# A hybrid decoder layer on one Trainium2 core: tiles of the phases, the input's squares, the sums of the left factors and the transposes of the merged rows moved

## The chip, the core and the metric

The kernel runs on one NeuronCore of a Trainium2 chip, in one launch. Five engines work beside each other, each in the order of its own instruction list: PE (TensorE) multiplies and transposes into PSUM, PEld loads its weights, DVE (VectorE) and ACT (ScalarE) do elementwise work, POOL (GpSimd) a little of it, and SP (SyncE) issues most DMAs; ACT's list holds DMA issues too. They wait for each other by semaphores. The metric is the device time of one execution in microseconds (us); here it is the median of three runs.

## The reference

One layer with SEQ = 256 tokens and D_MODEL = 4096, in float32:

```python
h = rms_norm(x, norm_gains)
z = h @ w_in            # GLA q,k,v,gate,decay | SWA q,k,v,gate | merge gates ga, gb
o_a = rms_norm(gla_mix(q, k, v, log_a), gla_norm_gains)    # 8 heads, chunks of 64, o_t = q_t S_t
y_a = (o_a * silu(gg)) @ w_gla_out                         # 2048 x 4096
o_b = swa_sink_mix(sq, sk, sv, sinks)                      # window 128, 32 query and 8 key heads
y_b = (o_b * silu(sg)) @ w_swa_out                         # 2048 x 4096
merged = sigmoid(ga + b0) * y_a + sigmoid(gb + b1) * y_b
x = x + merged @ w_out                                     # 4096 x 4096
return rms_norm(x, final_norm_gain)
```

## The kernel before, in words

**Products.** Every factor is split into a rounded part (hi) and a remainder (lo), and a product is three PE passes: hi·hi, hi·lo, lo·hi. For the weights ACT writes hi (`halves`, a CAST) and DVE writes lo (a TENSOR_TENSOR) for every raw tile of 512 KB that SP has fetched; `STG` (3) or `STM` (5) such hi and lo tiles exist, so a cast of a later tile waits until PE is done with an earlier one. One pass is a matmul of 128 x 128 by 128 x 512.

**Blocks (`gemm`).** The columns of `w_in` but the merge gates come in blocks of 512 (gq, gk, gv, gg for GLA; sk, sv, sq, sg for SWA); a block has 32 k-tiles, two token halves and so 192 matmuls. In the first block, gq, the input is fetched in pieces and `first_inputs` makes from each piece hT (ACT hi, DVE lo, 128 x 256 each, left factor of all blocks) and its squares: ACT squares 128 x 512, POOL adds them into `ssq` (L130).

**Pairs (`pair`).** The five large products (ya and yb out of the branches, ga and gb the merge gates, o the last one) go in pairs of 1024 columns, n = 0 to 3, with steps j of 256 rows of the weight (8 steps for ya and yb, 16 for the others). A step fetches two raw tiles r and s. In eight-form it takes 8 products (24 matmuls) into four accumulators q2, q3, q4, q8. In the steps of `SEVEN` it takes 7 products (21 matmuls): DVE forms sums t, u and s of the weight (L214 to L216), the left factor's sums lie ready in `xc`, and four more accumulators, q1, q5, q6, q7, take part. `combine` makes `xc` with six DVE operations and one ACT cast a step (L172 to L182). Pair 0 of each kind (ya0, yb0, ga0, o0) has eight-form alone, and `combine` stands behind it in the program.

**Ends of a pair (`outputs`).** In eight-form ACT copies the four accumulators (L262). In seven-form ACT copies q1, DVE forms v from q6 and two sums from q5 and q7, a third from q5, and adds q2, q3, q4, q8 (L247). PSUM has eight banks, so the next pair's first matmul into a bank waits until DVE or ACT has read it.

**Stages.** GLA (gq to gg), ya (spilled to DRAM), SWA (sk to sg), yb (spilled), then ga and gb alternately, whose sigmoids gate ya and yb into `m`; then the m stage: 16 groups of four PE transposes of m (m_t, L288), each split into `mT` by an ACT cast (L278) and a DVE subtraction (L279); then o0 to o3 with the residual x (`xt`) and, at the end, the root mean square over a row, the scaling and the writes. Staging tiles and work tiles of a stage lie in pools (`phase`) that are freed for the next; a new tile on the same memory waits for the old one's readers.

**Order.** A list scheduler places the instructions of each engine with its own estimates and the priorities `PRIO` (raw tiles and splits of blocks) and `PRM` (those of pairs); what stands where in a list is therefore not what the source reads like, and is shown below where it matters.

Of the kernel before, what the change touches and what calls it, by code (L numbers as in the profile page):

```python
# [49 lines left out]
def trunk_kernel(  # L50
# [59 lines left out]
    def first_inputs(gp, ssq):  # L110


        def before(k0, n):
# [74 lines left out]
    def pair(name, lhs, w, npr, xc=None, before=None, last=False):  # L188

        sev = SEVEN[npr] if xc is not None else ()  # L190
# [58 lines left out]
    def outputs(q, d, name, pool):  # L249

        if 1 in q:
# [5 lines left out]
            add(d[1][1], q[5], d[1][0], ALU.subtract)  # L257
        for t, i, b in ((0, 0, 2), (0, 1, 3), (1, 0, 4), (1, 1, 8)):
            if 1 in q:
                add(d[t][i], q[b], d[t][i])  # L260
            else:
                nc.scalar.copy(d[t][i], q[b])  # L262

    def spilled(name, lhs, w, dst, xc, pool):
# [237 lines left out]
    with phase("hl2") as cur["hl"], phase("swa") as sp:  # L502
# [35 lines left out]
        for i in range(4):  # L538
            qT = pairsT(f"sq{i}", zblock("sq", i), "qT")
            on = sp.tile([P, NT, NB], F32, tag="on", name=f"on{i}")  # L540
# [95 lines left out]
    mT = big.tile([P, KT, 2, S], F32R, tag="hT", name="mT")  # L636
    xcm = xp.tile([P, len(SEVEN[KT // 2]), 4, 2, P], F32R, tag="xc", name="xcm")
    st = ep.tile([P, NT, NBLK + 1], F32, tag="ev", name="st")
    for j in range(KT // 2):
        transpose_split(mT, 2 * j, m[:, :, 2 * j * P : 2 * (j + 1) * P], 2, f"m{j}")  # L640
    x2 = big.tile([P, NT, DM], F32, tag="oT", name="x2")
    for n in range(NP2):
        last = n == NP2 - 1
# [4 lines left out]
        outputs(q, [[x2[:, t, cs[i]] for i in range(2)] for t in range(NT)], f"o{n}", ep)
        gf = ep.tile([P, 2, NB], F32, tag="bt", name=f"gf{n}")
        nc.scalar.dma_start(gf, gfin[2 * n * NB : 2 * (n + 1) * NB].partition_broadcast(P).rearrange("p (i c) -> p i c", i=2))  # L650
        for t in range(NT):
            for i in range(2):
                xq = x2[:, t, cs[i]]
                xt = ep.tile([P, NB], F32, tag="yr", name=f"xt{n}{t}{i}", bufs=2)
                nc.scalar.dma_start(xt, x[t * P : (t + 1) * P, cs[i]])
                add(xq, xq, xt)
                nc.scalar.activation(xt, xq, AF.Square, accum_out=st[:, t, 2 * n + i : 2 * n + i + 1])  # L657
                add(xq, xq, gf[:, i, :], ALU.mult)
    for t in range(NT):
        sf = st[:, t, NBLK:]  # L660
        nc.vector.tensor_reduce(sf, st[:, t, :NBLK], AX.X, ALU.add)
        rms_scale(sf, sf, DM)
        for c in range(4):
            os = slice(c * 1024, (c + 1) * 1024)
            if c % 2 == 0:
                nc.vector.tensor_scalar(x2[:, t, os], x2[:, t, os], sf, None, ALU.mult)
# [77 lines left out]
```

## Time and profile before

| | us |
|---|---|
| median of 3 runs (2490.53 to 2492.29) | 2490.99 |
| profiled execution, its span | 2495.09, 2493.4 |
| PE busy | 2437.6 (98%), 10986 matmuls |
| DVE, ACT, POOL busy | 1724.6 (69%), 1225.4 (49%), 42.5 (2%) |
| mean DMA rate | 197 GB/s |

The profiled execution took 4.1 us more than the median of the runs, and 1.69 us of it lie around its span. PE is busy nearly all the time, so what can be won lies in matmuls left out, in the stops of PE and in stretches in which its clock is at the lower level.

### The profile page before, as it was taken

What the parts mean: (1) busy time and instruction counts of PE and PEld (TensorE: products, weight loads), DVE (VectorE), ACT (ScalarE), POOL (GpSimd) and SP (SyncE); (2) the same over time, 40 slices, a digit from 0 to 9 for tenths busy, and PEclk for the clock granted to TensorE, in tenths of its full rate; (3) what the DMA queues carried; (4) which work ended last, traced back from release to release, by engine and by line L of the source; (5) the groups of instructions that cost most, each with busy time, mean ns of one, the idle gap of its engine ahead of it and who ended that gap; (6) DMA issues with size and microseconds to landing.
All of it is one profiled execution on the core that took longest, in us unless ns stands there. A gap on an engine that the chain in (4) does not pass through costs nothing.

```text
span 2493.4 us, 29365 instructions
## 1 busy us (share of the span) xinstructions
PE 2437.6 (98%) x10986; PEld 1999.0 (80%) x10986; DVE 1724.6 (69%) x1929; ACT 1225.4 (49%) x1479; POOL 42.5 (2%) x52
## 2 busy tenths in 40 slices
PE   8999999999999999999989999999999999999997
PEld 6788888887877888888878788888888888788886
DVE  7465555445785455555557885799889988968886
ACT  6444444444543444445444444555555555545554
POOL 4000000000000000000000000000000000000000
PEclk9999999999999999999999999999999999999999
DMA  7556556556565655554556675677667676656665
GB/s 250 157 169 192 170 176 194 170 170 204 191 223 183 192 179 160 152 186 152 161 178 193 218 245 185 213 227 228 216 216 227 216 227 216 202 186 216 225 221 191
DMA packets 139024, 491.14 MB, mean 197 GB/s; under 512 B 15840, under 2 KB 16224, under 8 KB 138880
## 3 DMA queue, kind: packets, MB, share of 16 engines
q1 hardware_dynamic: 127296, 461.69, 58.4%
q10 hardware_dynamic: 11584, 27.57, 3.2%
q8 instruction: 86, 1.41, 0.2%
q14 instruction: 58, 0.48, 0.1%
HBM read 476.61 MB, written 12.58 MB: 196 GB/s over the span
## 4 chain that ended last, share of the span: by engine, by line
PE 89%; DVE 5%; issue 2%; DMA 2%; ACT 1%; POOL 0%; SPq 0%; ACTq 0%; POOLq 0%; DVEq 0%
PE ga_q L234 5%; PE ga_q L236 4%; PE ga_q L235 4%; PE gb_q L236 4%; PE gb_q L234 4%; PE gb_q L235 4%; PE o_q L236 4%; PE o_q L235 4%; PE o_q L234 4%; PE sg_a L163 2%; PE sg_a L162 2%; PE sq_a L164 2%; PE sq_a L163 2%; PE sq_a L162 2%; PE sg_a L164 2%; PE gg_a L164 2%
## 5 line engine op out<-in xcount | busy, mean ns | idle before, releaser
L214 DVE TENSOR_TENSOR gb_t<-gb_r,gb_s 128x1024 f32<-128x1024 f32 x24 | 29.3, 1221 | 11.0 <-DMA gb_s<-in_wgate_dram 11.0
L103 POOL TENSOR_TENSOR st<-st,mhalf 128x1 f32<-128x1 f32 x2 | 1.1, 553 | 1700.4 <-DVE st L102 1700.4
L565 ACT ACTIVATE s<-s,mx 128x128 f32<-128x128 f32 x64 | 28.4, 445 | 0.0
L214 DVE TENSOR_TENSOR o_t<-o_r,o_s 128x1024 f32<-128x1024 f32 x18 | 22.0, 1221 | 9.1 <-DMA o_s<-in_wout_dram 9.1
L130 POOL TENSOR_TENSOR ssq<-ssq,sq 128x512 f32<-128x512 f32 x15 | 26.4, 1757 | 25.3 <-ACT sq L129 24.7
L214 DVE TENSOR_TENSOR ga_t<-ga_r,ga_s 128x1024 f32<-128x1024 f32 x18 | 22.0, 1221 | 4.9 <-DMA ga_s<-in_wgate_dram 4.7
L121 DVE SCALAR_TENSOR_TENSOR hT<-xsb,gin_sb,hT 128x256 fp32r<-128x256 f32 x32 | 21.9, 733 | 4.9 <-ACT hT L120 4.9
L550 DVE SCALAR_TENSOR_TENSOR s<-s,mask 128x384 f32<-128x384 f32 x32 | 16.0, 552 | 6.0 <-PE s L549 6.0
L143 ACT CAST sg_16h<-sg_r 128x1024 fp32r<-128x1024 f32 x4 | 4.2, 1056 | 28.0 <-PE sg_a L164 28.0
L214 DVE TENSOR_TENSOR ya_t<-ya_r,ya_s 128x1024 f32<-128x1024 f32 x9 | 11.0, 1222 | 8.6 <-DMA ya_s<-in_wgla_dram 8.6
L214 DVE TENSOR_TENSOR yb_t<-yb_r,yb_s 128x1024 f32<-128x1024 f32 x9 | 11.0, 1222 | 8.4 <-DMA yb_s<-in_wswa_dram 8.4
L657 ACT ACTIVATE xt<-x 128x512 f32<-128x512 f32 x16 | 10.1, 630 | 13.7 <-DVE x L247 13.7
L216 DVE TENSOR_TENSOR gb_s<-gb_u,gb_s 128x512 f32<-128x512 f32 x24 | 16.5, 688 | 0.3
L215 DVE TENSOR_TENSOR gb_u<-gb_t,gb_r 128x512 f32<-128x512 f32 x24 | 16.5, 688 | 0.3
L473 DVE COPY oraw<-op 128x512 f32<-128x512 f32 x8 | 5.5, 692 | 15.6 <-PE op L472 15.6
L582 DVE COPY pT<-pt 128x384 f32<-128x384 f32 x16 | 8.9, 554 | 9.3 <-PE pt L579 9.3
L464 POOL TENSOR_SCALAR_AFFINE_SELECT ats<-ats 128x128 f32<-128x128 f32 x16 | 8.0, 523 | 415.4 <-DVE ats L462 415.4
L476 ACT ACTIVATE jk<-oraw 128x256 f32<-128x256 f32 x16 | 6.7, 418 | 16.9 <-DVE oraw L473 16.6
L579 PEld LDWEIGHTS pt<-ident,s 128*128 128x128 f32 x96 | 11.4, 145 | 4.4 <-ACT s L565 3.9
L120 ACT ACTIVATE hT<-xsb,gin_sb 128x256 fp32r<-128x256 f32 x32 | 14.1, 499 | 1.8 <-DMA xsb<-in_xT_dram 1.2
L579 PE MATMUL pt<-ident,s 128*128 128x128 f32 x96 | 14.9, 278 | 0.0
L288 PE MATMUL m_t<-ident,m 128*128 128x128 f32 x64 | 10.2, 302 | 3.7 <-DVE mT L279 3.7
(2816 smaller groups left out, 8954.8 us busy)
## 6 DMA issues: line engine op xcount, KB each, us to landing
gv_r<-in_win_dram SPq DMA_DIRECT2D x64, 512.0 KB, 3.8
gg_r<-in_win_dram SPq DMA_DIRECT2D x64, 512.0 KB, 4.0
sq_r<-in_win_dram SPq DMA_DIRECT2D x64, 512.0 KB, 3.6
sg_r<-in_win_dram SPq DMA_DIRECT2D x64, 512.0 KB, 3.7
ga_r<-in_wgate_dram SPq DMA_DIRECT2D x64, 512.0 KB, 4.7
ga_s<-in_wgate_dram SPq DMA_DIRECT2D x64, 512.0 KB, 5.1
gb_r<-in_wgate_dram SPq DMA_DIRECT2D x64, 512.0 KB, 4.6
gb_s<-in_wgate_dram SPq DMA_DIRECT2D x64, 512.0 KB, 5.4
```

Source lines behind the costliest of these rows:

```text
L121: nc.vector.scalar_tensor_tensor(hT[:, kt, 1, :], xsb[:, kt, :], g, hT[:, kt, 0, :].bitcast(F32), ALU.mult, ALU.subtract)
L130: nc.gpsimd.tensor_tensor(ssq, ssq, sq, ALU.add)
L162: nc.tensor.matmul(acc[t], lh, hi[:, i, :], start=kt == 0, stop=False)
L163: nc.tensor.matmul(acc[t], lh, lo[:, i, :], start=False, stop=False)
L164: nc.tensor.matmul(acc[t], ll, hi[:, i, :], start=False, stop=kt == nkt - 1)
L214: nc.vector.tensor_tensor(ts, r1, r2[:, 0:1, :].broadcast_to([P, 2, NB]), ALU.add)
L215: nc.vector.tensor_tensor(t2[:, 0, :], ts[:, 1, :], r1[:, 0, :], ALU.add)
L234: nc.tensor.matmul(q[i], lh, hi[:, c, :], start=done[i] == 1, stop=False)
L235: nc.tensor.matmul(q[i], lh, lo[:, c, :], start=False, stop=False)
L236: nc.tensor.matmul(q[i], ll, hi[:, c, :], start=False, stop=done[i] == total[i])
L565: nc.scalar.activation(s4[:, k, cs], s4[:, k, cs], AF.Exp, bias=mx[:, k, t : t + 1], accum_out=sm[:, k, t : t + 1],)
L579: nc.tensor.transpose(tp[:, m * P : (m + 1) * P], s4[:, k, m * P : (m + 1) * P], ident)
```

## The change

The tiles that a stage still needs in its last instructions move to pools of their own: `glo` takes gng_sb, oraw, ss, gt from GLA's pool, `slo` takes on, sg from SWA's. `mixed_staging` claims the staging tiles of ya and yb in a fixed order at the stage's start. The input's squares are emitted inside the second block (gk) instead of the first. Pair 0 of ya, yb and ga takes seven-form from step 5 (ya, yb) or 8 (ga) on, and `combine` is spread over its steps 1 to 3 or 1 to 6. Of the 16 groups of transposes of m, 12 are emitted inside `outputs` of gb3, before its last four sums; the other four come in steps 2 to 5 of o0, and o's `combine` in its steps 9 to 14. In o's pairs x comes in one DMA a pair and is added before the accumulator of the last sum instead of after it. In o3 the products of q8 come last; the scaling of the last 512 columns takes the final gain with it; a row's output goes in six pieces instead of four.

```diff
+        def squares(k0, n):
             xr = xsb[:, k0 : k0 + n, :]
-            if k0 < KW:
-                nc.scalar.activation(ssq[:, k0 : k0 + n, :], xr, AF.Square)
+            if k0 == 0:
+                nc.scalar.activation(ssq, xr, AF.Square)
                 return
...
+    def mixed_staging():
+
+        cur["n"], cur["r"] = STM, 6
+        for tag, n, dt, bufs in (("hi", 2, F32R, STM), ("raw", 2, F32, 6), ("t2", 1, F32, 1), ("t13", 2, F32, 1), ("lo", 2, F32R, STM)):
+            cur["hl"].tile([P, n, NB], dt, tag=tag, name=f"first_{tag}", bufs=bufs)
...
-    def pair(name, lhs, w, npr, xc=None, before=None, last=False):
+    def pair(name, lhs, w, npr, xc=None, before=None, last=False, since=0):
 
-        sev = SEVEN[npr] if xc is not None else ()
+        sev = [j for j in SEVEN[npr] if j >= since] if xc is not None else ()
...
-                work.sort(key=lambda x: x[0] in (4, 8))
+                work.sort(key=lambda x: {4: 1, 8: 2}.get(x[0], 0))
...
+        if between is not None:
+            between()
         for t, i, b in ((0, 0, 2), (0, 1, 3), (1, 0, 4), (1, 1, 8)):
             if 1 in q:
+                if extra is not None:
+                    add(d[t][i], d[t][i], extra[t][i])
                 add(d[t][i], q[b], d[t][i])
+            elif extra is not None:
+                add(d[t][i], q[b], extra[t][i])
             else:
                 nc.scalar.copy(d[t][i], q[b])
 
+    def first_pair(lhs, xc, npr, name, order, since, n):
+
+        if n > 0:
+            return {}
+
+        def before(j):
+            if 1 <= j <= len(order):
+                combine(lhs, xc, SEVEN[npr], name, at=order[j - 1])
+
+        return {"before": before, "since": since}
...
-        q0 = zblock("gq", 0, before=first_inputs(gp, ssq), chunks=RAMP)
-        k0 = zblock("gk", 0)
+        load, squares = first_inputs(gp, ssq)
+        q0 = zblock("gq", 0, before=load, chunks=RAMP)
+        k0 = zblock("gk", 0, before=squares)
...
+    def merged():
+
+        mTs.append(big.tile([P, KT, 2, S], F32R, tag="hT", name="mT"))
+        for j in range(3 * KT // 8):
+            transpose_split(mTs[0], 2 * j, m[:, :, 2 * j * P : 2 * (j + 1) * P], 2, f"m{j}")
...
+    sums = lambda j: (
+        combine(mT, xcm, SEVEN[KT // 2], "m", at=j - 9) if j >= 9
+        else transpose_split(mT, 2 * (j + 10), m[:, :, 2 * (j + 10) * P : 2 * (j + 11) * P], 2, f"m{j + 10}") if 2 <= j < 6
+        else None
+    )
...
+    for t in range(NT):
+        nc.vector.tensor_scalar(sf[t], st[:, t, NBLK - 1 : NBLK], 1.0 / DM, sf[t], ALU.mult, ALU.add)
+        nc.gpsimd.tensor_tensor(sf[t], sf[t], mhalf[:, 0:1], ALU.pow)
+        at = 0
+        for c, w in enumerate((512, 512, 1024, 1024, 512, 512)):
```

**Place one: ACT near the end of the first block.** gq_24h to gq_28h are casts of the first block's weights, hT makes the left factor of the input's pieces, sq are the squares. Before:

```order
L143 CAST gq_24h<-gq_r_420 128x1024
L129 ACTIVATE sq_391<-xsb 128x512
L129 ACTIVATE sq_417<-xsb 128x512
L337 DMA bdec_sb<-in_bdec_dram 128x8
L129 ACTIVATE sq_442<-xsb 128x512
L143 CAST gq_26h<-gq_r_445 128x1024
L120 ACTIVATE hT<-xsb,gin_sb 128x256 x4
L143 CAST gq_28h<-gq_r_471 128x1024
L129 ACTIVATE sq_468<-xsb 128x512
```

With the change:

```order
L145 CAST gq_24h<-gq_r_385 128x1024
L131 ACTIVATE sq_701<-xsb 128x512
L131 ACTIVATE sq_722<-xsb 128x512
L365 DMA gng_sb<-in_gng_dram 128x256
L145 CAST gq_26h<-gq_r_407 128x1024
L120 ACTIVATE hT<-xsb,gin_sb 128x256 x4
L131 ACTIVATE sq_743<-xsb 128x512
L145 CAST gq_28h<-gq_r_430 128x1024
L131 ACTIVATE sq_764<-xsb 128x512
```

The square sq_442, which stood ahead of the cast gq_26h, stands behind that cast and behind the four hT operations (as sq_743); the other squares shown keep theirs, although the source has them in the next block.

**Place two: PE at the passage from SWA to yb.** ob_t are the eight transposes of the last SWA rows, yb_q the accumulators of yb0, yb_r0h and yb_r0l the two parts of its first weights, obT the left factor. Before:

```order
L288 MATMUL ob_t_9266<-ident,on_8819 128x128
L288 MATMUL ob_t_9273<-ident,on_8819 128x128
L288 MATMUL ob_t_9266<-ident,on_8819 128x128 x3
L288 MATMUL ob_t_9273<-ident,on_8819 128x128 x3
L234 MATMUL yb_q_9292<-yb_r0h,obT 128x512
L234 MATMUL yb_q_9294<-yb_r0h,obT 128x512
L234 MATMUL yb_q_9293<-yb_r0h,obT 128x512
L235 MATMUL yb_q_9292<-yb_r0l,obT 128x512
```

With the change (the first row is the first transpose):

```order
L313 MATMUL ob_t_9297<-ident,on_8850 128x128
L313 MATMUL ob_t_9304<-ident,on_8850 128x128
L244 MATMUL yb_q_9333<-yb_r0h,obT 128x512
L244 MATMUL yb_q_9335<-yb_r0h,obT 128x512
L244 MATMUL yb_q_9334<-yb_r0h,obT 128x512
L244 MATMUL yb_q_9336<-yb_r0h,obT 128x512
L245 MATMUL yb_q_9333<-yb_r0l,obT 128x512
L246 MATMUL yb_q_9333<-yb_r0h,obT 128x512
L245 MATMUL yb_q_9335<-yb_r0l,obT 128x512
L313 MATMUL ob_t_9297<-ident,on_8850 128x128 x3
L313 MATMUL ob_t_9304<-ident,on_8850 128x128 x3
L246 MATMUL yb_q_9335<-yb_r0h,obT 128x512
```

Seven matmuls of yb now stand between the second transpose and the other six. On ACT the casts of yb_r0, yb_s0 and yb_r1 likewise stand ahead of the two casts of obT, which they followed before.

**Place three: DVE at the passage from gb3 to o0.** gb_d holds gb3's rows (L247 sums and products, L627 gate), m the merged rows, o_r1l, o_s1l and o_r2l are remainders of o0's first weights, mT is the transposed left factor of o. Before:

```order
L247 TENSOR_TENSOR gb_d_16018<-gb_q_15379,gb_d_16018 128x512
L144 TENSOR_TENSOR o_s1l<-o_s_16211,o_s1h 128x1024
L247 TENSOR_TENSOR gb_d_16018<-gb_q_15378,gb_d_16018 128x512
L247 TENSOR_TENSOR gb_d_16018<-gb_q_15380,gb_d_16018 128x512
L247 TENSOR_TENSOR gb_d_16018<-gb_q_15381,gb_d_16018 128x512
L627 SCALAR_TENSOR_TENSOR gb_d_16018<-gb_d_16018,rstd,bt_15372 128x512 x3
L247 TENSOR_TENSOR gb_d_16018<-gb_d_16018,ygb_16029 128x512
L247 TENSOR_TENSOR gb_d_16018<-gb_d_16018,ygb_16035 128x512
L247 TENSOR_TENSOR m<-m,gb_d_16018 128x512 x2
L627 SCALAR_TENSOR_TENSOR gb_d_16018<-gb_d_16018,rstd,bt_15372 128x512
L279 TENSOR_TENSOR mT<-m_t_16056,mT 128x2x256
```

With the change:

```order
L257 TENSOR_TENSOR gb_d_16115<-gb_q_15476,gb_d_16115 128x512
L146 TENSOR_TENSOR o_s1l<-o_s_16280,o_s1h 128x1024
L257 TENSOR_TENSOR gb_d_16115<-gb_q_15475,gb_d_16115 128x512
L257 TENSOR_TENSOR gb_d_16115<-gb_q_15477,gb_d_16115 128x512
L146 TENSOR_TENSOR o_r2l<-o_r_16321,o_r2h 128x1024
L304 TENSOR_TENSOR mT<-m_t_16123,mT 128x2x256
L304 TENSOR_TENSOR mT<-m_t_16130,mT 128x2x256
L304 TENSOR_TENSOR mT<-m_t_16137,mT 128x2x256
L304 TENSOR_TENSOR mT<-m_t_16144,mT 128x2x256
L304 TENSOR_TENSOR mT<-m_t_16151,mT 128x2x256
L304 TENSOR_TENSOR mT<-m_t_16158,mT 128x2x256
L304 TENSOR_TENSOR mT<-m_t_16165,mT 128x2x256
```

The first remainder of mT stood behind the whole chain of gate, product and sum of gb3; now 12 of them stand right behind three of its four accumulator sums, and that chain comes after them.

## Rows read from the trace of the kernel before

**Rows 1.** The page's chain that ended last: shares of the span by engine.

```profile
PE 89%; DVE 5%; issue 2%; DMA 2%; ACT 1%; POOL 0%; SPq 0%; ACTq 0%; POOLq 0%; DVEq 0%
```

**Rows 2.** Waits of PE: waiting line <- what ended it: us, times, longest.

```profile
PE yb_q L234 <- DVE yb_d L247: 4.1, 2, 2.5
PE yb_q L234 <- ACT yb_r0h L143: 3.9, 1, 3.9
PE ya_q L234 <- ACT ya_r0h L143: 3.9, 1, 3.9
PE ya_q L234 <- DVE ya_d L247: 3.4, 2, 2.0
...
PE gq_a L163 <- DVE gq_28l L144: 1.8, 1, 1.8
...
PE yb_q L235 <- DVE yb_t2l L144: 0.8, 2, 0.4
```

**Rows 3.** Stretches: length, busy of PE, PEld, DVE, ACT, POOL (instructions), clock, DMA, GB/s.

```profile
640.00:660.00 20.00, 20.00 (x90) 16.57 (x89) 14.98 (x15) 12.90 (x15) 0.00 (x0) 1.00 0.73 249
55.94:59.35 3.41, 3.41 (x10) 2.66 (x9) 0.80 (x1) 0.87 (x1) 0.00 (x0) 0.50 0.77 288
591.83:602.07 10.24, 6.32 (x18) 4.53 (x18) 9.54 (x19) 6.41 (x8) 0.00 (x0) 0.50 0.85 289
1277.91:1288.15 10.24, 6.26 (x17) 4.58 (x18) 9.09 (x19) 6.38 (x9) 0.00 (x0) 0.50 0.67 204
2134.65:2141.48 6.83, 5.08 (x18) 4.13 (x19) 6.78 (x11) 2.85 (x4) 0.00 (x0) 0.50 0.66 218
1372.00:1375.40 3.40, 0.94 (x5) 0.48 (x3) 3.40 (x6) 1.22 (x2) 0.00 (x0) 1.00 0.65 186
```

**Rows 4.** Timeline of ACT and DVE, first block: start, us, operation [idle before <- releaser].

```profile
45.82 0.63 ACT L129 ACTIVATE sq<-xsb 128x512 f32<-128x512 f32 x1 [2.06 <-POOL ssq L130]
46.36 1.03 ACT L143 CAST gq_26h<-gq_r 128x1024 fp32r<-128x1024 f32 x1
52.17 2.29 DVE L144 TENSOR_TENSOR gq_28l<-gq_r,gq_28h 128x1024 fp32r<-128x1024 f32 x1
```

**Rows 5.** Timeline of ACT and PE at the passage from GLA to ya.

```profile
595.40 0.62 ACT L181 CAST xca<-yad 128x512 fp32r<-128x512 f32 x1 [1.69 <-DVE yad L180]
595.93 1.04 ACT L143 CAST ya_r0h<-ya_r 128x1024 fp32r<-128x1024 f32 x1
597.02 1.65 PE L234 MATMUL ya_q<-ya_r0h,oaT 128*128 128x512 f32 x3 [3.92 <-ACT ya_r0h L143]
```

**Rows 6.** Timeline of ACT and PE at the passage from SWA to yb.

```profile
1275.71 0.69 ACT L597 ACTIVATE sg<-sg_a,rstd 128x512 f32<-128x512 f32 x1 [1.60 <-DVE on L599]
1277.97 1.54 PE L288 MATMUL ob_t<-ident,on 128*128 128x128 f32 x6 [1.79 <-DVE on L599]
1282.34 1.04 ACT L143 CAST yb_r0h<-yb_r 128x1024 fp32r<-128x1024 f32 x1
1283.43 1.65 PE L234 MATMUL yb_q<-yb_r0h,obT 128*128 128x512 f32 x3 [3.92 <-ACT yb_r0h L143]
```

**Rows 7.** Timeline of SP's queue and DVE at the passage from ya1 to ya2.

```profile
676.29 0.33 SPq L210 DMA_DIRECT2D ya_s<-in_wgla_dram  x1
682.14 1.23 DVE L214 TENSOR_TENSOR ya_t<-ya_r,ya_s 128x1024 f32<-128x1024 f32 x1 [2.33 <-DMA ya_s<-in_wgla_dram]
```

**Rows 8.** Timeline of PE at the passage from gb3 to o0.

```profile
2136.40 1.12 PE L288 MATMUL m_t<-ident,m 128*128 128x128 f32 x4 [3.69 <-DVE mT L279]
```

**Rows 9.** Timeline at the passage from o1 to o2: PE's first matmul of o2, then DVE.

```profile
2312.57 0.39 PE L234 MATMUL o_q<-o_t0h,xcm 128*128 128x512 f32 x1
2315.65 1.22 DVE L144 TENSOR_TENSOR o_s1l<-o_s,o_s1h 128x1024 fp32r<-128x1024 f32 x1
2316.78 1.22 DVE L144 TENSOR_TENSOR o_r2l<-o_r,o_r2h 128x1024 fp32r<-128x1024 f32 x1
```

**Rows 10.** DMA rate in 40 equal slices of the stretch from 2476 to 2494 us.

```profile
GB/s 0 0 64 232 332 369 141 27 146 428 400 401 419 382 410 410 419 392 410 391 55 0 246 400 428 373 419 382 410 410 410 392 401 373 27 9 0 0 0 0
```

More of the change, by code (lines that the diff above doesn't have):

```diff
@@ L90, in trunk_kernel @@
     make_identity(nc, ident)
-    gin_sb = const.tile([P, KT], F32, name="gin_sb")
+    gin_sb = const.tile([P, KT], F32, tag="kt", name="gin_sb")
     nc.scalar.dma_start(gin_sb, gin)
@@ L130, in before @@
             nc.gpsimd.tensor_tensor(ssq, ssq, sq, ALU.add)
-        return before
+        return before, squares
     PRIO = 400
@@ L165, in gemm, with combine @@
         return acc
-    def combine(lhs, xc, js, name):
+    def mixed_staging():
+        cur["n"], cur["r"] = STM, 6
+        for tag, n, dt, bufs in (("hi", 2, F32R, STM), ("raw", 2, F32, 6), ("t2", 1, F32, 1), ("t13", 2, F32, 1), ("lo", 2, F32R, STM)):
+            cur["hl"].tile([P, n, NB], dt, tag=tag, name=f"first_{tag}", bufs=bufs)
+    def combine(lhs, xc, js, name, at=None):
         for c, j in enumerate(js):
+            if at is not None and at != c:
+                continue
             a = cur["hl"].tile([P, 2, NT, P], F32, tag="t2", name=f"{name}a{j}")
@@ L247, in add, with outputs @@
         nc.vector.tensor_tensor(o, a, b, op)
-    def outputs(q, d, name, pool):
+    def outputs(q, d, name, pool, extra=None, between=None):
         if 1 in q:
@@ L337, in trunk_kernel @@
         nc.scalar.dma_start(bdec_sb, bdec)
-        gng_sb = gp.tile([P, DV], F32, name="gng_sb")
+        gng_sb = glo.tile([P, DV], F32, name="gng_sb")
         nc.scalar.dma_start(gng_sb, gng.partition_broadcast(P))
@@ L539, in trunk_kernel @@
             qT = pairsT(f"sq{i}", zblock("sq", i), "qT")
[L540 removed]
+            on = slo.tile([P, NT, NB], F32, tag="on", name=f"on{i}")
             for a in range(2):
@@ L616, in trunk_kernel @@
             nc.scalar.dma_start(bt, bgates[w, 2 * n * NB : 2 * (n + 1) * NB].partition_broadcast(P).rearrange("p (i c) -> p i c", i=2))
-            q = pair(f"{kind}{n}", hT, wgate[w * NP2 + n], KT // 2, xc=None if n + w == 0 else xch)
-            if n + w == 0:
-                combine(hT, xch, SEVEN[KT // 2], "h")
+            q = pair(
+                f"{kind}{n}", hT, wgate[w * NP2 + n], KT // 2, xc=xch,
+                **first_pair(hT, xch, KT // 2, "h", (3, 4, 5, 0, 1, 2), 8, n + w),
+            )
             d = ep.tile([P, NT, 2, NB], F32, tag="ev", name=f"{kind}_d{n}")
-            outputs(q, [[d[:, t, i, :] for i in range(2)] for t in range(NT)], f"{kind}{n}", ep)
+            mt = merged if w == 1 and n == NP2 - 1 else None
+            outputs(q, [[d[:, t, i, :] for i in range(2)] for t in range(NT)], f"{kind}{n}", ep, between=mt)
             for t in range(NT):
@@ L653, in trunk_kernel @@
                 xq = x2[:, t, cs[i]]
[L654 to L658, printed above, removed]
-    for t in range(NT):
[L660 to L666, printed above, removed]
+                nc.scalar.activation(xt[:, t, i, :], xq, AF.Square, accum_out=st[:, t, 2 * n + i : 2 * n + i + 1])
+                if not last or i == 0:
+                    add(xq, xq, gf[:, i, :], ALU.mult)
+                if last and i == 0:
+                    nc.vector.tensor_reduce(sf[t], st[:, t, : NBLK - 1], AX.X, ALU.add)
+                    nc.vector.tensor_scalar(sf[t], sf[t], 1.0 / DM, EPS, ALU.mult, ALU.add)
+    for t in range(NT):
+        nc.vector.tensor_scalar(sf[t], st[:, t, NBLK - 1 : NBLK], 1.0 / DM, sf[t], ALU.mult, ALU.add)
+        nc.gpsimd.tensor_tensor(sf[t], sf[t], mhalf[:, 0:1], ALU.pow)
+        at = 0
+        for c, w in enumerate((512, 512, 1024, 1024, 512, 512)):
+            os = slice(at, at + w)
+            at += w
+            if at == DM:
+                nc.vector.scalar_tensor_tensor(x2[:, t, os], x2[:, t, os], sf[t], gf[:, 1, :], ALU.mult, ALU.mult)
+            elif c % 2 == 0:
+                nc.vector.tensor_scalar(x2[:, t, os], x2[:, t, os], sf[t], None, ALU.mult)
             else:
-                nc.scalar.activation(x2[:, t, os], x2[:, t, os], AF.Copy, scale=sf)
+                nc.scalar.activation(x2[:, t, os], x2[:, t, os], AF.Copy, scale=sf[t])
             nc.sync.dma_start(out[t * P : (t + 1) * P, os], x2[:, t, os])
```

42 lines of the change are left out of this document (22 added, 20 removed).

## The prediction, made before the changed kernel ran

> **What bounds the kernel now.** The first view is the chain that ended last: PE holds 89% of it, DVE 5% [rows 1]. PE also works in nearly all of the span, so time is won only by matmuls left out, by stops of PE, and by stretches at its lower clock level. The second view, the waits of PE, gives the stops that the change touches [rows 2]: at the passages from GLA to ya and from SWA to yb 3.9 us each (the first cast of the new weights ends them), and at pair changes, where a bank of PSUM waits for DVE (ya_q 3.4 and yb_q 4.1 us, two times each). The third, the table of stretches, gives PE's pace: 20 us of undisturbed seven-form hold 90 matmuls; two are cut by the edges, so one takes about 0.226 us [rows 3]. It also shows DVE at 15.0 and ACT at 12.9 us of these 20, so both have room in steady work. And it shows where the granted clock is 0.50, the level of 1.2 GHz: around 55.9 behind the stop for gq_28l, around 592 and 1278 about the two passages, around 2135 about the stop of the m stage. A stretch that PE fills at that level returns half its length if it goes. The last views are the timelines at these places [rows 4 to 9].
>
> **Seven-form in the first pairs.** Five steps change from 24 to 21 matmuls: step 5 of ya0 and yb0, steps 8, 10 and 13 of ga0. That is 15 matmuls x 0.226 = **-3.4**. Their sums t, u and s and the spread `combine` go to DVE and ACT, which hide them by the room above; without it, three sums and one remainder too many would cost PE some 3 us a step.
>
> **Two new stops at pair changes.** ya0 and yb0 now end with q5, q6 and q7 in use, so ya0 to ya1 becomes what ya1 to ya2 is. What is late there: SP issues ya_s at 676.29, when a raw tile comes free; DVE waits 2.33 us for it and forms t at 682.14 [rows 7], and the reads of q6 and q7 stand behind t in DVE's list, with PE behind them. The order there is the same at ya0 to ya1 now. The price is the mean of the old stops [rows 2]: 3.4/2 for ya and 4.1/2 for yb, and 0.4 behind each for t2l (shown at yb, taken alike at ya): 2.1 + 2.45 = **+4.5**. Below it would be 0, if the raw tile comes free earlier; above, +5.8 with the longest ones (2.0, 2.5) and 0.6 each. The stop at 1372 lies at clock 1.00 [rows 3], so I add no lower clock.
>
> **The first block.** ACT waited 2.06 us for POOL's adds before a square at 45.82, and the cast gq_26h stood behind it at 46.36 [rows 4]. Now the cast is ahead of that square and starts some 2 us earlier, as then does what follows it on ACT and DVE: gq_28l ends near 52.4 instead of 54.46. PE stopped 1.8 us for it [rows 2], so it asked near 52.7. The stop goes, and with it the stretch from 55.94, full of matmuls at 0.50: half of 3.41 is 1.7 [rows 3]. Together **-3.5**. This has no slack: with DVE's gq_28l at 2.29 us, twice the 1.13 of the same shape later [rows 4, 9], a late square elsewhere may eat it. Bounds: +2 (one more such stop) to -6 (the first block's other stop, of about this size, goes too). I take the middle one, which the row of the blocked cast supports.
>
> **GLA to ya.** ACT waited 1.69 us for yad, did xca at 595.40 and then ya_r0h at 595.93; PE resumed at 597.02 [rows 5]. Now ya_r0h stands ahead of xca, and its raw tile and staging tile are free, so it starts where ACT's wait began: 595.40 - 1.69 = 593.7. PE resumes at 594.8, **-2.2**. Bounds: -1.1, if the lower clock lasts until 602.07 all the same (2.2 us more at half pace), and -4.7, if it never falls ((602.07 - 597.02)/2 = 2.5 more).
>
> **SWA to yb.** PE resumed at 1283.43 because yb_r0h stood behind the two casts of obT and these behind all eight transposes [rows 6]. Now the cast stands behind the last sigmoid sg (1275.71 before). A DVE operation of yb's `combine`, ahead of the rows' last products, waits for the last sg matmul and delays that sigmoid by about 1.1 us (two operations of 128x512, about 0.6 each as worked out below), to end near 1277.5; with 1.04 for the cast PE starts yb at 1278.6, 4.8 earlier. Six transposes, which before filled the wait, now come among the first matmuls: before, six took 1.54 us at the lower clock [rows 6], half of it at the higher, so 0.7. Sum **-4.1**, with as much time at the lower clock as before. Bounds: -1.7, if that stretch still lasts until 1288.15 (2.4 more at half pace), and -6.5 without it (4.7/2 = 2.4 less).
>
> **The m stage.** PE stopped 3.69 us before the four transposes at 2136.40, for a bank that DVE reads [rows 8]; the stop lies in a stretch of 6.83 us at 0.50, with 5.08 of PE's work in it [rows 3]. Now 12 of the 16 groups come before gb3's last sums, between o0's first matmuls, and DVE forms their remainders in a row. A remainder takes about 0.6 us (half of the 1.13 from start to start of one twice as wide, [rows 9]). PE's list puts in about one group of four transposes and a matmul per remainder, some 0.7 us at full clock, so it is not far ahead of DVE: I leave 0.3 for small waits. What is late next is gb3's gate chain, which ends before PE reaches the last four groups in steps 2 to 5. Sum -3.7 - 5.08/2 + 0.3 = **-5.9**. Bounds: -2, if PE runs into DVE again and the clock falls as before; -6.5.
>
> **The pairs of o.** The additions of x now stand before the sums of q2 to q8. From s1l at 2315.65 DVE has four operations of 1.13 us and three of 0.6 until q4 is read (2322.0), four more until q8 is (2324.4) [rows 9]. PE's list brings the matmul that needs a read bank as the 43rd and 54th of o2; from 2312.57 with 0.226 that is 2322.1 and 2324.6. It just fits; 0.2 each at o1 to o2 and o2 to o3 make **+0.4**. Bounds: -0.5 and +3.
>
> **The tail.** The rate of DMA falls to 55, 0 and 246 GB/s in three slices of 0.45 us between the writes of the two rows [rows 10]. With x added early and six pieces the second row follows closely: **-0.8**, the first two slices. Bounds: 0 and -3.
>
> The sum is -3.4 + 4.5 - 3.5 - 2.2 - 4.1 - 5.9 + 0.4 - 0.8 = -15.0. Against the profiled execution, 2495.1, that is 2480.1. It stands 4.1 above the median of the runs shown, and I take that off: **2476.0**.
>
> **Rivals.** *The first block gains nothing* (2479.5): POOL's 15 adds and DVE's work are the same as before, and where they meet decides. For it: the doubled gq_28l [rows 4]; against: the cast that decides is no longer behind POOL. The Trainium skill, "SBUF — State Buffer", section "SBUF: two separate sides", says that a DVE operation with two SBUF inputs and a GpSimd one that reads SBUF take the shared ports as an exclusive lock, the other blocking for a whole instruction. By that rule the blocked time would be moved and not removed, and the time is this rival's; the doubled row agrees, but which engine held what no row here shows.
>
> *Half of the gains* (2484.0): the clock still falls at the m stage (+2.5), the first block gains nothing (+3.5), and the lower clock at SWA to yb lasts as long as before (+2). For it: lower clock stands beside each of these stops now [rows 3]; against: two of the three stops lose their cause.
>
> *No lower clock at the two passages either* (2471.5): -2.5 and -2. For it: the stops shrink from 3.9 to under 3 us; against: the clock was already at 0.50 at 591.83 and 1277.91, before the wait for the cast began [rows 3, 5, 6].
>
> *Late banks with lower clock* (2496.0, the slower side): DVE holds q6, q7 or the late q4 and q8 behind sums that wait for a DMA, at every pair change with seven-form behind it. ya0 and yb0 then cost 2.5 more each (the half of 5.08 at 0.50), and ga0 to gb0, o1 to o2 and o2 to o3 each a stop of 2.5 (the longest of rows 2) and 2.5 behind it: 5 + 15 = 20. It decides from 15. For it: the stop of 1.8 was followed by the lower clock; against: those of 2.0 and 2.5 at pair changes were not [rows 2, 3]. [...]
>
> **How the numbers follow.** Forecast 0.45 (own range 2472 to 2481), first block unchanged 0.13, half of the gains 0.20, no lower clock 0.12, late banks 0.10. A measurement of this kernel can tell about 0.2%, 5.0 us, from no change: faster is below 2486.0. The forecast, the first rival and the third are all faster; of half the gains 0.14 is and 0.06 is not; of the late banks 0.05 is the same and 0.05 slower. Faster 0.84, same 0.11, slower 0.05. The range is 2469 to 2487: below by the larger bounds of the tail and the passages, above by half the gains and 3 us.
>
> **What would show it.** Right: the waits for gq_28l and mT gone; three waits for ya_d and yb_d instead of two; PE back some 1.7 us after its last work at GLA to ya, and on yb within 3 us of the transposes' first wait; no stretch at 0.50 near 56 and 2135; waits for o's sums near zero; no hole in the tail's writes; 15 matmuls fewer. Wrong: new stretches at 0.50 behind pair changes, or a wait of o_q for x above 1 us, or gq_28l still ended late.

## The result, and the profile after

The changed kernel takes **2479.1 us** (median of 5 runs, 2477.8 to 2480.9) against 2491.0 of the kernel before in the same comparison. The ratio is 0.995, with an interval of 0.9936 to 0.9965: 0.5% faster, 11.9 us. The forecast was 2476.0 with a range of 2469 to 2487, so the time lies inside; 3.1 us of the expected gain are missing.

The profiled execution of the changed kernel took 2479.1 us, just its median, and that of before 2495.1, 4.1 above its median. So the two traces differ by 16.0 us and the medians by 11.9. The table has the first matmul of a stage in either trace, as PE's timeline gives it, and what was won up to there; "second" is another profile of the kernel before, from the first experiment.

| first matmul of | before | second | after | after against before | against second |
|---|---|---|---|---|---|
| gk (end of the first block) | 61.53 | 57.96 | 59.42 | -2.1 | +1.5 |
| ya0 | 597.02 | 593.12 | 592.18 | -4.8 | -0.9 |
| ya2 (behind ya0 and ya1) | 684.62 | 681.04 | 681.30 | -3.3 | +0.3 |
| sg3 | 1217.23 | 1212.39 | 1212.36 | -4.9 | 0.0 |
| yb1 | 1329.39 | 1323.55 | 1319.70 | -9.7 | -3.9 |
| yb2 | 1370.87 | 1365.03 | 1365.03 | -5.8 | 0.0 |
| gb0 | 1547.80 | 1540.59 | 1538.63 | -9.2 | -2.0 |
| o0 | 2130.61 | 2123.39 | 2121.66 | -9.0 | -1.7 |
| o1 | 2229.61 | 2222.67 | 2214.45 | -15.2 | -8.2 |
| last matmul | 2478.90 | 2471.32 | 2464.04 | -14.9 | -7.3 |
| end of the span | 2493.4 | 2485.8 | 2477.4 | -16.0 | -8.4 |

Against the first profile the gains come where the forecast put them. Against the second the first block gains nothing, and the new stop at yb0 to yb1 has eaten what the passage from SWA won (it lies behind yb1's first matmuls, so it shows in the row of yb2). The lower clock of single executions is in these rows too.

The waits of PE in the changed kernel, to hold against [rows 2]:

```profile
PE yb_q L244 <- DVE yb_d L257: 4.8, 3, 2.0
PE ya_q L244 <- DVE ya_d L257: 4.6, 3, 1.7
PE gq_a L165 <- DVE gq_12l L146: 2.9, 1, 2.9
...
PE gq_a L165 <- DVE gq_28l L146: 1.2, 1, 1.2
PE yb_q L244 <- ACT yb_r0h L145: 1.2, 1, 1.2
PE ya_q L245 <- DVE ya_t2l L146: 1.2, 3, 0.4
PE ya_q L244 <- ACT ya_r0h L145: 1.0, 1, 1.0
PE yb_q L245 <- DVE yb_t2l L146: 0.8, 2, 0.4
```

The two passages' waits fell from 3.9 to about 1 us each and the wait of m_t is gone. The banks at pair changes are waited for three times each instead of two. In the first block the wait for gq_28l is smaller and not gone, and one of 2.9 for gq_12l is new.

DVE shows why gq_28l is still late. Its four hT operations and gq_28l, first in the kernel before (its gq_28l is in [rows 4]), then in the changed one:

```profile
49.55 2.70 DVE L121 SCALAR_TENSOR_TENSOR hT<-xsb,gin_sb,hT 128x256 fp32r<-128x256 f32 x4
```

```profile
48.10 4.78 DVE L121 SCALAR_TENSOR_TENSOR hT<-xsb,gin_sb,hT 128x256 fp32r<-128x256 f32 x4
52.80 1.21 DVE L146 TENSOR_TENSOR gq_28l<-gq_r,gq_28h 128x1024 fp32r<-128x1024 f32 x1
```

The cast gq_26h does start 2.4 us earlier (43.95 instead of 46.36), but hT takes 2.1 us longer, and gq_28l ends at 54.0 instead of 54.46.

The passage from GLA to ya (ACT, ACT, PE) and from SWA to yb (ACT, ACT, PE), to hold against [rows 5, 6]:

```profile
590.60 0.59 ACT L303 CAST oaT<-oa_t 128x512 fp32r<-128x512 f32 x1 [2.69 <-PE oa_t L313]
591.08 1.05 ACT L145 CAST ya_r0h<-ya_r 128x1024 fp32r<-128x1024 f32 x1
...
592.18 1.65 PE L244 MATMUL ya_q<-ya_r0h,oaT 128*128 128x512 f32 x3 [0.98 <-ACT ya_r0h L145]
```

```profile
1271.77 0.69 ACT L623 ACTIVATE sg<-sg_a,rstd 128x512 f32<-128x512 f32 x1 [2.52 <-DVE on L625]
1272.35 1.03 ACT L145 CAST yb_r0h<-yb_r 128x1024 fp32r<-128x1024 f32 x1
...
1273.44 2.07 PE L244 MATMUL yb_q<-yb_r0h,obT 128*128 128x512 f32 x4 [1.21 <-ACT yb_r0h L145]
```

The cast follows at once on the last sigmoid or the first cast of oaT, as forecast, and PE resumes 1.1 us after it starts.

Stretches of the changed kernel, with the columns of [rows 3]:

```profile
29.78:33.19 3.41, 3.41 (x10) 2.62 (x9) 3.41 (x6) 0.38 (x1) 0.00 (x0) 0.50 0.64 217
589.56:596.39 6.83, 5.85 (x17) 4.44 (x17) 6.42 (x14) 5.79 (x8) 0.00 (x0) 0.50 0.46 139
...
1272.23:1279.05 6.82, 5.61 (x16) 4.64 (x17) 6.32 (x8) 4.58 (x7) 0.00 (x0) 0.50 0.37 112
1323.43:1326.84 3.41, 3.41 (x9) 2.68 (x9) 3.41 (x4) 1.04 (x1) 0.00 (x0) 0.50 0.59 169
2121.00:2131.00 10.00, 10.00 (x64) 8.56 (x63) 9.86 (x17) 6.77 (x14) 0.00 (x0) 1.00 0.35 113
```

The lower clock stays at the passages, 6.8 us long where it was 10.2. It is gone at o0's start (the last row, at 1.00), where it lasted 6.83 us before. It is new behind the stop at yb0 to yb1 (1323.43).

The last stretch of DMA, of the same length as in [rows 10] and from 2461 on:

```profile
GB/s 0 0 0 0 0 0 0 0 168 373 378 437 382 419 410 400 391 364 382 378 396 369 373 423 401 410 401 428 391 360 382 387 132 5 0 0 0 0 0 0
```

The hole between the two rows' writes is closed; from the last matmul to the end it is 13.4 us instead of 14.5.

### The profile page after: what moved, and what is told of

The parts are those of the page before. It is cut to its first block, busy times and chain, and to the rows that moved or that the text cites. A ratio compares the mean times of both kernels' runs of the same rounds, so it can differ in the third digit from the quotient of the medians.

```text
span 2477.4 us, 29374 instructions
## 1 busy us (share of the span) xinstructions
PE 2429.8 (98%) x10971; PEld 1992.3 (80%) x10971; DVE 1759.8 (71%) x1982; ACT 1223.5 (49%) x1475; POOL 41.7 (2%) x52
## 4 chain that ended last, share of the span: by engine, by line
PE 89%; DVE 5%; DMA 2%; issue 2%; ACT 1%; POOL 0%; SPq 0%; DVEq 0%; POOLq 0%; ACTq 0%
PE ga_q L245 5%; PE ga_q L244 5%; PE ga_q L246 4%; PE gb_q L245 4%; PE gb_q L244 4%; PE gb_q L246 4%; PE o_q L244 4%; PE o_q L245 4%; PE o_q L246 4%; PE sg_a L165 2%; PE sg_a L164 2%; PE sg_a L166 2%; PE sq_a L165 2%; PE sq_a L164 2%; PE sq_a L166 2%; PE gg_a L166 2%
## 5 line engine op out<-in xcount | busy, mean ns | idle before, releaser
L132 POOL TENSOR_TENSOR ssq<-ssq,sq 128x512 f32<-128x512 f32 x15 | 25.6, 1705 | 24.9 <-ACT sq L131 24.4
L257 DVE TENSOR_TENSOR ya_d<-ya_q,ya_d 128x512 f32<-128x512 f32 x20 | 12.9, 685 | 5.2 <-PE ya_q L246 5.1
L605 PE MATMUL pt<-ident,s 128*128 128x128 f32 x96 | 14.9, 278 | 0.2
L226 DVE TENSOR_TENSOR ga_s<-ga_u,ga_s 128x512 f32<-128x512 f32 x21 | 14.5, 689 | 0.4
```

What stands on the lines that cost most here:

```text
L226: nc.vector.tensor_tensor(r2[:, 0, :], t2[:, 0, :], r2[:, 1, :], ALU.add)
L605: nc.tensor.transpose(tp[:, m * P : (m + 1) * P], s4[:, k, m * P : (m + 1) * P], ident)
```

## The experiments

Ten runs follow: the kernel before again, and nine edits of the changed kernel. The ratios are to the kernel before, timed beside each; "to after" is the difference of medians to 2479.1. The kernel before itself had medians of 2491.0 to 2492.3 in these comparisons, so a difference of about 1 us says nothing.

| run | median us | to after | ratio, interval |
|---|---|---|---|
| the kernel before again | 2492.0 | +12.9 | 0.9999 (0.999 to 1.0007) |
| squares in the first block again | 2480.3 | +1.2 | 0.9951 (0.9938 to 0.9965) |
| transposes of m behind gb3 again | 2483.6 | +4.5 | 0.9967 (0.9955 to 0.998) |
| old pools again | 2486.2 | +7.1 | 0.9978 (0.9969 to 0.9987) |
| ya0 and yb0 in eight-form | 2474.5 | -4.6 | 0.9932 (0.992 to 0.9945) |
| squares after the first block, adds on DVE | 2473.8 | -5.3 | 0.9927 (0.9914 to 0.9939) |
| adds on DVE, squares not moved | 2472.6 | -6.5 | 0.9922 (0.991 to 0.9935) |
| 8 raw tiles in ya | 2478.1 | -1.0 | 0.9946 (0.9932 to 0.9959) |
| sums ahead of t | 2464.6 | -14.5 | 0.9888 (0.9873 to 0.9903) |
| sums ahead of t, and squares after | 2458.8 | -20.3 | 0.9864 (0.9851 to 0.9878) |

**The kernel before, a second profile.** No edit.

> The kernel before, unchanged, for a second profile and more times. Theory A (the lower clock differs from one execution to the next): the profiled execution of before (2495.1) stood 4.1 us above its median because it had one or two stretches at 0.50 that most executions lack; a new profile lies within 2 us of 2491, its mean clock is 0.992 or more instead of 0.990, and at least one of the stretches at 35, 56, 776 or 2135 is shorter or missing while the stops of PE stay (within 0.3 us each). Theory B (profiling adds the time): the new profile is at 2494 to 2496 again with the same stretches.

The profile took 2487.5 us at a mean clock of 0.993; its 11 runs lie between 2487.5 and 2496.4. Its longest waits of PE behind the start-up, and the stretch where the first profile had its second drop of the clock:

```profile
PE yb_q L234 <- ACT yb_r0h L143: 4.2, 1, 4.2
PE ya_q L234 <- ACT ya_r0h L143: 4.1, 1, 4.1
PE m_t L288 <- DVE mT L279: 3.7, 1, 3.7
PE ya_q L234 <- DVE ya_d L247: 3.0, 2, 1.7
...
PE gq_a L163 <- DVE gq_16l L144: 1.9, 1, 1.9
...
PE yb_q L234 <- DVE yb_d L247: 1.5, 1, 1.5
```

```profile
50.00:60.00 10.00, 9.81 (x43) 7.80 (x42) 6.80 (x8) 3.73 (x4) 0.35 (x1) 1.00 0.67 214
```

Theory A holds in that executions differ, and it did not go far enough: the profile lies 3.5 below 2491 where A allowed 2, and the stops differ as well as the clock. The stop for gq_28l, from which the forecast took 3.5 us, has shrunk to 0.2, and the stops at yb's pair changes are 1.7 and 1.8 us from start to start instead of 2.8 and 2.0. The stops at the passages and the m stage are nearly as they were; the lower clock is again 10.2 us at GLA to ya and 6.8 at the m stage, but 6.8 instead of 10.2 at SWA to yb. B falls: profiling adds no fixed time.

**The parts undone.** Squares back in the first block:

```diff
-        q0 = zblock("gq", 0, before=load, chunks=RAMP)
-        k0 = zblock("gk", 0, before=squares)
+        q0 = zblock("gq", 0, before=lambda k, n: (load(k, n), squares(k, n)), chunks=RAMP)
+        k0 = zblock("gk", 0)
```

> The changed kernel with the input's squares emitted in the first block again, as before. Theory A (the move of the squares gains nothing over executions: the stop for gq_28l and its lower clock, which the forecast took away for 3.5 us, are missing in the second profile of the kernel before too, and in the changed kernel a stop of 2.9 for gq_12l stands in their place): gk starts between 58 and 62, and the median is 2478 to 2481. Theory B (the term of 3.5 us was right): gk starts at 61 or later and the median is 2481.5 to 2484.

2480.3, and gk starts at 58.1. Theory A: the difference of 1.2 us is not resolved (the ratios to the kernel before are 0.9951 and 0.995). The traces with POOL's adds and without a stretch at 0.50 in the first block say the same: gk starts at 58.0 (the kernel before, second profile) and 58.1 (this run) with the squares in the first block, and at 58.8 and 58.5 (the next two runs) with the squares moved.

All 16 groups of transposes behind gb3 again (`between=mt` and the groups in o0's steps left out, `merged` over `range(KT // 2)` called before o0):

> The changed kernel with all 16 groups of transposes of m behind gb3 again; the sums of o's left factor stay spread over o0. Theory A (stop and lower clock both came from the transposes' wait): a wait m_t of 3.7, a stretch at 0.50 at o0's start, and +5.9: 2484 to 2486. Theory B (only the stop, the clock falls anyway): +3.5, 2482 to 2483.

2483.6, +4.5, between the two theories' numbers. The mechanism of A holds: the wait and the lower clock are both back in its trace:

```profile
PE m_t L313 <- DVE mT L304: 3.7, 1, 3.7
```

```profile
2126.65:2133.48 6.83, 5.24 (x18) 4.25 (x19) 6.80 (x11) 2.87 (x5) 0.00 (x0) 0.50 0.59 179
```

From the first matmul of o0 to that of o1 this trace takes 99.1 us, both traces of the kernel before 99.0 and 99.3, and the changed kernel 92.8. A stretch at 0.50 at o0's start stands in all three traces with the transposes behind gb3 and in none of the other nine.

The old pools:

```diff
-        gng_sb = glo.tile([P, DV], F32, name="gng_sb")
+        gng_sb = gp.tile([P, DV], F32, name="gng_sb")
...
-            on = slo.tile([P, NT, NB], F32, tag="on", name=f"on{i}")
+            on = sp.tile([P, NT, NB], F32, tag="on", name=f"on{i}")
```

> The changed kernel with gng_sb, oraw, ss, gt in GLA's pool and on, sg in SWA's again; the fixed order of the staging tiles stays. In this list yb_r0h and ya_r0h stand behind the casts of obT, oaT and xc again. Theory A (the pools make the first casts early, and these set both passages): waits of 3.5 us or more at ya_r0h and yb_r0h, +2.5 and +4.9 at the starts of ya and yb: 2485 to 2488. Theory B (the clock gives it back): under +3, 2480 to 2482.

2486.2, +7.1, theory A, and both waits are back:

```profile
PE ya_q L244 <- ACT ya_r0h L145: 4.5, 1, 4.5
PE yb_q L244 <- ACT yb_r0h L145: 4.2, 1, 4.2
```

So the casts are early only with the new pools: the fixed order of the staging tiles does not do it alone. Whether the pools would do it without that order no run shows.

ya0 and yb0 in eight-form, the sums of the left factors still spread:

```diff
-            q = pair(f"{name}{n}", lhs, w[n], OKT // 2, xc=xc, **first_pair(lhs, xc, OKT // 2, name, (2, 0, 1), 5, n))
+            q = pair(f"{name}{n}", lhs, w[n], OKT // 2, xc=xc, **first_pair(lhs, xc, OKT // 2, name, (2, 0, 1), OKT, n))
```

> The changed kernel, but ya0 and yb0 have eight-form alone again, with the sums of the left factors still spread over their steps. Theory A (the new stops cost more than the six matmuls save): +1.4 for the matmuls, -2.4 for the stop at ya0 to ya1, -2.1 for that at yb0 to yb1 and -1.7 where a lower clock followed it; the median is 2474 to 2477. Theory B (the stops only move on to the next pair change): the median is 2480 to 2481.

2474.5, 4.6 faster than the changed kernel, theory A. Each pair kind is back at two stops (yb_d 4.2, ya_d 3.1 us in its trace). The six matmuls save 1.4 us at 0.226 each, so by the medians the stops that they bring cost about 6. In the traces, from the first matmul of ya1 to that of ya2 the changed kernel takes 44.2 us and this run 41.5, from yb1 to yb2 45.3 and 41.5: 2.7 and 3.8 more, the second with a stretch of 3.41 us at 0.50 in it.

**What makes the new stops.** In the changed kernel at ya0 to ya1 (DVE, DVE, PE):

```profile
634.26 1.23 DVE L224 TENSOR_TENSOR ya_t<-ya_r,ya_s 128x1024 f32<-128x1024 f32 x1 [1.96 <-DMA ya_s<-in_wgla_dram]
...
639.48 0.69 DVE L257 TENSOR_TENSOR ya_d<-ya_q,ya_v 128x512 f32<-128x512 f32 x1
...
640.31 0.47 PE L244 MATMUL ya_q<-ya_u0h,xca 128*128 128x512 f32 x1 [1.67 <-DVE ya_d L257]
```

DVE stands 1.96 us before t, and the sum that frees the bank comes 5.2 us after t's start. Two edits tell apart what is at fault, the tile or the order. The first gives the sums of q5 to q7 of ya and yb, and ACT's copy of q1 that they start from, a priority ahead of t:

```diff
+            with tc.high_priority(early):
                 nc.scalar.copy(d[0][0], q[1])
                 add(v, q[6], d[0][0])
                 add(d[0][1], q[5], v, ALU.subtract)
                 add(d[1][0], q[7], v)
                 add(d[1][1], q[5], d[1][0], ALU.subtract)
```

(`early` is 200 for ya and yb, and 0 elsewhere.)

> The changed kernel, but at the ends of the pairs of ya and yb the sums of q5, q6 and q7 have a higher priority, so they stand ahead of the next pair's t in DVE's list. Theory A (the banks are late because their sums stand behind a t that waits for its raw tile): the waits ya_d and yb_d (4.6 and 4.8 us) fall below 1.5 together, the waits for t2l (2.0) stay or shrink, the lower clock behind the stop at yb0 to yb1 goes, and the median is 2468 to 2472. Theory B (the raw tile itself is what PE needs): PE stops for t0l or t2l instead for as long, and the median stays at 2477 to 2480.

2464.6, 14.5 us faster. Theory A in the mechanism, but its 2468 to 2472 was too high: the waits of 4.6 + 4.8 + 2.0 in the changed kernel's trace and half of the 3.41 us at 0.50 behind yb0 to yb1 make 13.1, and where the rest comes from is not shown. The sums of q5 and q7 at ya0 to ya1 stand ahead of that t now (634.26 above, 635.57 here):

```profile
628.33 1.28 DVE L258 TENSOR_TENSOR ya_d<-ya_q,ya_v 128x512 f32<-128x512 f32 x2
...
635.57 1.23 DVE L225 TENSOR_TENSOR ya_t<-ya_r,ya_s 128x1024 f32<-128x1024 f32 x1
```

In its trace PE has no stop of over 1 us at a pair change of ya or yb; of its waits there one row stays in the first dozen, and DVE still waits for the same DMAs:

```profile
PE ya_q L246 <- DVE ya_t2l L147: 0.6, 3, 0.3
```

```profile
DVE ya_t L225 <- DMA ya_s<-in_wgla_dram: 12.1, 3, 4.4
...
DVE yb_t L225 <- DMA yb_s<-in_wswa_dram: 10.2, 3, 3.7
```

DVE's waits for these DMAs are up to 4.4 us long, and PE's stops there are 0.3 us each at most: the sums no longer stand behind them.

The second edit gives ya 8 raw tiles instead of 6 (`mixed_staging(8)` there):

> The changed kernel with 8 raw tiles instead of 6 in the stage of ya alone, so that SP can fetch the next pair's weights earlier; DVE's order is otherwise not given another priority. Theory A (t waits because its raw tile comes free late, and the sums behind it wait with it): DVE's waits for DMA ya_s at the pair changes fall from 2 to under 0.5 us, the waits ya_d from 4.6 to under 1.5, yb's stay at 4 to 6.5; median 2474 to 2476. Theory B (DVE's load alone makes the sums late): ya_d stays above 3 and the median at 2478 to 2481.

Neither theory as written. ya_d is gone from PE's waits, as A said, but the median stays near 2478, as B said, because other waits took its place (yb_d belongs to yb, which this edit leaves alone):

```profile
PE ya_q L245 <- DVE ya_s2l L146: 3.9, 3, 1.6
PE yb_q L244 <- DVE yb_d L257: 3.9, 3, 1.6
...
PE ya_q L245 <- DVE ya_r3l L146: 2.4, 3, 0.8
```

```profile
649.34 1.23 DVE L224 TENSOR_TENSOR ya_t<-ya_r,ya_s 128x1024 f32<-128x1024 f32 x1 [4.58 <-DMA ya_s<-in_wgla_dram]
650.48 1.22 DVE L146 TENSOR_TENSOR ya_s2l<-ya_s,ya_s2h 128x1024 fp32r<-128x1024 f32 x1
```

With more tiles the scheduler places a later t early in DVE's list; there it waits 4.58 us for its own DMA, and s2l, which PE needs, stands behind it. More room moved the stop here and did not remove it.

**What sets the first block.** Squares tied to its end and added by DVE:

```diff
+        one = gp.tile([P, 1], F32, name="one")
+        nc.vector.tensor_scalar(one, q0[0][:, 0:1], 0.0, 1.0, ALU.mult, ALU.add)
...
-            nc.scalar.activation(sq, xr, AF.Square)
-            nc.gpsimd.tensor_tensor(ssq, ssq, sq, ALU.add)
+            nc.scalar.activation(sq, xr, AF.Square, scale=one)
+            nc.vector.tensor_tensor(ssq, ssq, sq, ALU.add)
```

> The changed kernel, but the input's squares are tied to the end of the first block (they read a scale of 1 that is formed from its accumulator) and DVE adds them instead of POOL. Theory A (POOL's adds slow DVE in the first block: hT x4 takes 5.9, 3.7 and 4.8 us there): hT x4 falls to about 2 us, the waits for gq_12l (2.9) and gq_28l (1.2) and the stretch at 0.50 near 30 go, gk starts at 54 to 56 instead of 59.4, and the median is 2473 to 2476. Theory B (the DMA of the first block sets its length, 257 GB/s): gk starts at 58.5 to 59.5 and the median stays at 2478 to 2480.

And with the adds on DVE alone (the last of these lines), without the scale, so that the squares stay where they are:

> The changed kernel with the squares where they are and their 15 adds on DVE instead of POOL, so DVE has some 9 us more to do before gk's first tiles. Theory A (POOL's adds stretch DVE's operations; that sets the first block): hT x4 takes 1.7 us each as in the run with the squares after the block, gk starts at 52 to 55, median 2473 to 2476. Theory B (the squares on ACT in front of the casts set it): hT x4 is short but gk starts at 58 or later, median 2477 to 2481.

2473.8 and 2472.6; gk starts at 52.4 and 53.0, in the first run earlier than A said. Theory A in both, and since in the second the squares stay where they were, it is POOL's adds and not ACT's squares. POOL in the changed kernel, then DVE's hT, four operations, in the changed kernel, with the squares after, and with the adds on DVE:

```profile
18.49 4.30 POOL L132 TENSOR_TENSOR ssq<-ssq,sq 128x512 f32<-128x512 f32 x2 [5.58 <-ACT sq L131]
23.02 4.14 POOL L132 TENSOR_TENSOR ssq<-ssq,sq 128x512 f32<-128x512 f32 x3 [0.23 <-ACT sq L131]
```

```profile
21.55 5.90 DVE L121 SCALAR_TENSOR_TENSOR hT<-xsb,gin_sb,hT 128x256 fp32r<-128x256 f32 x4
```

```profile
19.78 1.67 DVE L121 SCALAR_TENSOR_TENSOR hT<-xsb,gin_sb,hT 128x256 fp32r<-128x256 f32 x4
```

```profile
21.49 1.67 DVE L121 SCALAR_TENSOR_TENSOR hT<-xsb,gin_sb,hT 128x256 fp32r<-128x256 f32 x4
```

The same four take 5.90 us beside POOL's adds and 1.67 without, and gq_12l, for which PE then stops 2.9 us, stands right behind them. An add takes 0.69 us on DVE and 1.55 (median) on POOL. Fifteen adds more on DVE, some 10 us of work, cost less than what POOL's adds hold up.

**Both together.**

> The changed kernel with both edits: the sums of q5, q6, q7 of ya and yb ahead of the next pair's t, and the squares after the first block with their adds on DVE. Theory A (the two places are apart and their gains add up): 2479.1 - 14.5 - 5.3, so 2457 to 2462. Theory B (what is won in the first block is lost again at a later stop or in lower clock, as the squares run alone stopped 6.4 and 5.5 us at yb_d and ya_d): 2463 to 2466.

2458.8, near the sum of the two (2479.1 - 14.5 - 5.3 = 2459.3). Theory A. It beats both kernels: 1.36% under the kernel before (interval 1.22 to 1.49%), 0.8% under the changed one by the medians.

## Why the prediction was right, and which steps were not

- **The first block failed** (-3.5). The rival that had it gain nothing (2479.5) came nearest to the time. The row on which the term stood, the cast behind a square that waits for POOL, was real, and the cast came 2.4 us earlier as forecast. The step that failed is the next one, that what follows the cast on DVE comes earlier by as much: hT took 4.78 us instead of 2.70 beside POOL's adds, and gq_28l ended at 54.0, not near 52.4. The stop of 1.8 us and its lower clock also belong to one execution: the second profile of before has 0.2 there, and undoing the move costs 1.2, which is not resolved. DVE and POOL meet at other operations now (gq_12l, 2.9). The rule of the Trainium skill weighed at that rival ("SBUF — State Buffer", section "SBUF: two separate sides") fits what the runs show: with the adds in the block their price moves from one operation to the next, and without them it goes (four hT operations 5.90 and 1.67 us). Which engine held the ports at a given moment no row shows.
- **The passages were right in mechanism** and about right in size: -2.2 and -4.1 were forecast, undoing the pools gives +7.1. Lower clock stayed there for 6.8 us each in the changed kernel.
- **The m stage was right**: wait and lower clock went together and come back together. -5.9 was forecast; from o0 to o1 the two traces have -6.2, and undoing it gives +4.5 in the medians, so the size is uncertain by some 1.5.
- **The new stops were right in place and cause and too cheap.** +4.5 less 2 x 0.68 for six matmuls makes +3.1 net; undoing seven-form there gives 4.6. The forecast left the lower clock out because the stop at 1372 had none. That step failed: both profiles of before have no stretch at 0.50 at a pair change of ya or yb, but of the seven traces that have the new stops (the changed kernel and the runs that change neither the first pairs nor the order of the sums) five have one or two, of 3.41 or 6.83 us. In the changed kernel's it costs half of 3.41 behind the stop at yb0 to yb1. The run with eight-form has one too, at yb2 to yb3, so the sizes do not close to the last us.
- **ga0 and the tail** came out: 2.0 us for nine matmuls between ga0 and gb0, and -1.1 against -0.8 for the tail. The pairs of o cost +0.5 and +0.2 up to o2 and o3, with no wait of PE at the pair changes, against +0.4.
- **The step from the profile to the median counted something twice.** Taking off 4.1 applies the sum of -15.0 to the median. That is sound only for gains that every execution has. Most of the 4.1 is what one execution of before happened to have: its first block ended 3.6 us later than that of the second profile. So the stop and the lower clock there came off once as a gain (-3.5) and once within the 4.1. With either left out the forecast would have been 2479.5 or 2480.1.

The parts as measured, -1.2 for the squares, -7.1 for the pools, -4.5 for the transposes, +4.6 for ya0 and yb0 (medians of the runs that undo them) and -2.0 for ga0, +0.7 for o and -1.1 for the tail (traces), make -10.6 of the 11.9 us.

Two of the signs that the prediction named for being wrong did appear: gq_28l ended late, and a stretch at 0.50 stands behind a pair change. So the range held although the first block's term was wrong and the new stops were too cheap: those two misses, 2.3 and 1.5 us, are small beside the 11 us that the range leaves above 2476.0. Two slips in the working move nothing: 2.0, 2.5 and twice 0.6 make 5.7, not 5.8, and half of 1.54 is 0.8, not 0.7.

The rival with half of the gains missed in its main condition, as the lower clock at the m stage did go; that the first block gains nothing held. The one without lower clock at the passages missed. Late banks with lower clock happened at one pair change in the changed kernel's trace, yb0 to yb1, and not at those of ga or o.

## What to carry to other kernels

A wait on an engine off the critical path costs what stands behind it in that engine's list. Look for the operations that free a bank or a buffer and put them ahead of any that may wait for a DMA; more buffers alone (8 raw tiles instead of 6) only let the scheduler put another waiting operation in front here. Before a stop is booked as a gain, see it in a second profile: a stop that is only in one execution is no term of the sum.

## What was not expected of the hardware

- POOL's adds of 128x512 stretch the DVE operations beside them up to 3.5 times (5.90 against 1.67 us for four), though POOL is busy for only 2% of the span (its 15 adds, 25.6 us busy, all lie between 11 and 52.2 us).
- A stop of nearly the same length is followed by lower clock in one run and not in another. The stop for gq_12l is 2.9 us long in the changed kernel, with 0.50 behind it (29.78, above), and as long in the run with the old pools, where the clock stays at 1.00 from 28 to 38 us. In the changed kernel the one at yb0 to yb1, 2.35 us from start to start, was (1323.43, above). With the squares after the first block the stops at yb0 to yb1 and yb1 to yb2, 2.23 and 2.70, were not; the stretches from their beginning on:

```profile
1312.94:1318.00 5.06, 3.22 (x14) 2.15 (x13) 5.06 (x7) 2.27 (x3) 0.00 (x0) 1.00 0.65 198
...
1357.33:1367.33 10.00, 7.32 (x31) 5.26 (x30) 9.65 (x13) 3.19 (x5) 0.00 (x0) 1.00 0.73 248
```

What decides between the two stays open.
